# Attention of a one-core hybrid step: low scores over all 128 rows, value products of both heads side by side, context scores padded with zeros

## The chip, the cores and the metric

The kernel runs on one core of one Trainium2 chip. The metric is the device time in microseconds (us) of one execution, and the time of a kernel is the median of its runs. The engines are named as in the profile: PE is TensorE's matmuls, PEld its weight loads, DVE is VectorE, ACT is ScalarE, POOL is GpSimd and SP is SyncE, whose queue issues nearly all DMAs. A matmul has a stationary operand, which a weight load brings into the array, and a moving operand, whose columns are streamed through. The array has 128 rows (the contracted dimension) and 128 columns (the partitions of the output).

## The reference, cut to what matters

One inference step of a two-layer network over 512 latent tokens and 128 context tokens, D = 1024, everything in float32. Each layer is a half FFN, a token mixer and a half FFN. The mixer of layer 0 is a Fourier mixer, that of layer 1 is attention with 16 heads of 64 channels, and the change is in that attention alone.

```
q, k, v = split(h @ w_qkv)             # q scaled by 64 ** -0.5
# 128 context queries: dense over the 128 context keys of this step
p = softmax(q_ctx @ k_ctx.T);  o_ctx = p @ v_ctx
# 512 latent queries (grid of 8 rows x 64 columns): one softmax over
#   the 8 x 16 keys of the neighbourhood (plus a relative-position bias per head)
#   and the 128 cached context keys (no bias)
logits = concat([q @ k_win.T + bias, q @ cache_k.T])
o = softmax(logits) @ concat([v_win, cache_v])
```

The step also returns the context keys and values.

## The kernel before

**Layout.** Activations lie transposed: channels on the 128 partitions, tokens along the free dimension. The latent tokens are ordered column by column of the grid, so that a block of 128 neighbouring tokens needs the keys of two neighbouring 128-key tiles and the tile of cached keys: 384 keys in all, of which the bias masks those outside the window.

**Precision.** A float32 product of projections is three matmuls of a rounded kind (F32R, a reduced float32 that TensorE streams in one pass): an operand x is split into hi (x rounded) and lo (x minus hi), and `mm3` (lines 208 to 210) adds hi·hi, hi·lo and lo·hi. The split of a weight unit of 128x1024 is one ACT operation (L191) and one DVE operation (L193). Matmuls whose operands are plain F32 (transposes aside: values, context scores) show as two instructions each in the profile.

**The attention, stage by stage.** Heads are taken in eight pairs c; a pair has its 128 channels on the 128 partitions, head p0 = 0 on rows 0 to 63 and p0 = 1 on rows 64 to 127.

- `qk(c)` projects q and k of a pair: 4 x 8 triples of `mm3`, 320 columns each. `query` (L908, L916) and `key` (L933, L936) take the results out of PSUM. For head p0 the query tile holds the hi part on the head's own 64 rows and the lo part on the other 64. The key tile holds the hi part on the head's own rows, and `double` (L946) copies it to the other rows. So one matmul over 128 rows gives q_hi·k_hi + q_lo·k_hi. The lo part of the keys of both heads lies in one tile (`low`, the right part of `pair[0]`), on each head's own rows only.
- `v_tiles(quad, ts)` projects the values, 256 channels at a time; four quads, five token tiles each.
- `pair_parts(c, ...)` lists the work of a pair's attention as small parts. `scores(p0, b)` makes the scores of head p0 and query block b: the 128-row matmul L1038, then L1039, which takes q_hi (64 rows) with the lo keys (64 rows), both 384 columns into the same bank; then the softmax: L1042 on DVE (bias, maximum), L1024 DVE, L1025 ACT (exponential and its sum), L1026 and L1027 DVE. `turn` transposes the 128x384 weights in three steps on TensorE (L1052) into the one `turn` bank, and ACT copies them out (L1054). `values(p0, b)` (L1065) multiplies them with the values: stationary 128x64, so 64 columns of the array, the half that belongs to the head. `ctx_scores` (L1073, 64 rows) and `ctx_values` (L1088) do the same for the context queries.

**Order.** In `before` the jobs of a pair are the four blocks of head 0, the four of head 1, then the two of the context; at each step of the list stand the scores of job n, the turn of job n-1 and the values of job n-2, thirty parts in all. `weave` spreads the parts of pair c over the `mm3` triples of the projections of pair c+1 (and of a value quad, after c = 0, 3 and 5): `tick` adds a nominal time for each triple and takes the next part when its due time has come; `flush` emits what is left. After the flush `behind` appends three or four jobs of the modulation of later layers: each loads a 128x1024 tile and runs two products over it on DVE (L348). The last pair is woven into the first part of the output projection. The framework writes all waits and sets the order of each engine's queue; every engine takes its queue in order.

**Buffers that matter here.** PSUM: four `main` banks, two `score`, one `turn`, one `sum` (where the values of a pair are summed, and taken out by L1068 and L1090). SBUF: four `left` (softmax), three `right` (transposed weights), and four `raw` tiles, through which every weight unit, every modulation tile and every bias tile (L1032, `raw_tile`) passes. The DMA of a raw tile is issued on SP at L156 when its buffer is free.

Of the kernel before, what the change touches and what calls it, by code (L numbers as in the profile page):

```python
# [18 lines left out]
P = 128  # L19
# [28 lines left out]
TEMPS = {"square": (2, TOK), "total": (2, TOK), "rms": (2, HALF), "left": (4, 384), "right": (3, 384)}  # L48
# [9 lines left out]
KL = 512  # L58
QUERY_SEGS = (((0, HALF, 64),), ((HALF, 448, HALF + 64), (448, LAT, 0)))
KEY_SEGS = (((0, 256, 0), (256, HALF, 640)), ((HALF, 384, 640 + HALF - 256), (384, LAT, 512)))  # L60
BLOCK_KEYS = (slice(0, 5, 2), slice(0, 3), slice(1, 6, 2), slice(5, 2, -1))
BLOCK_BIAS = (slice(0, 7, 3), slice(1, 4), slice(1, 6, 2), slice(1, 4))
TAKEN = (
    ((0, 448, 64, ((1, None), (2, 3))), (64, 0, 64, ((0, 0), (1, None)))),
    ((0, 64, P, ((0, 0), (1, 1), (2, None))),),
    ((0, 192, P, ((0, 1), (1, None), (2, 2))),),
    ((0, 320, P, ((0, 2), (1, 3), (2, None))),),
# [11 lines left out]
def queries(pair, p0):  # L79
    return pair[1][:, 768:] if p0 else pair[0][:, :LAT]  # L80
# [29 lines left out]
class Kernel:  # L110
# [296 lines left out]
    def inverse_rms(self, acc):  # L407

        nc = self.nc
        final = type(acc) is list  # L410
        if not final:
            spare = acc[:, 1, :1]
            nc.vector.tensor_tensor(acc[:, 0], acc[:, 0], acc[:, 1], op=ALU.add)
            acc = [acc[:, 0]]
        nc.scalar.activation(self.col(1), acc[0][:, :1] if final else spare, AF.Sqrt)
        if not final:
            yield 1800
        in_turn = lambda: self.tc.issue_after(self.latest.ins) if self.latest else ExitStack()
        ps = self.bank("sum")
        cuts = (0, P, HALF - P)  # L420
        with in_turn():
            for j, t in enumerate(cuts):
                nc.tensor.matmul(ps[:, j : j + 1], acc[0][:, t : t + P], self.ones[:, :1], start=True, stop=True)  # L423
        col = self.col(3)
        nc.scalar.activation(col, ps[:, :3], AF.Sqrt, bias=self.eps, scale=1.0 / D)
        nc.vector.reciprocal(col, col)
        yield 1800
        ps = self.bank("sum")
        with in_turn():
            for j, t in enumerate(cuts):  # L430
                self.spread = nc.tensor.matmul(ps[:, t : t + P], col[:, j : j + 1].to_broadcast([P, P]), self.ident,  # L431
                                               start=True, stop=True)
        r = self.temp("rms")
# [455 lines left out]
    def attention(self, base, boundary):  # L889
# [13 lines left out]
        def query(c, half, ps):  # L903
# [6 lines left out]
            if half:  # L910
                ctx_qk[c] = self.temp("rms")
                nc.scalar.activation(ctx_qk[c][:, :P], ps[:, LAT - HALF : HALF], AF.Copy, scale=HD ** -0.5)
# [6 lines left out]
        def cached(c):  # L919
            low = pairs[c][0][:, KL:]  # L920
            for p0, (rows, other) in enumerate(sides):
                cache = self.cache[0][rows, c * P : (c + 1) * P].unsqueeze(1).to_broadcast([64, 2, P])
                two = lambda t: t[rows, 2 * P : 4 * P].rearrange("p (c t) -> p c t", c=2)
                k = two(pairs[c][1 + p0])
                nc.scalar.activation(k, cache, AF.Copy)
                nc.gpsimd.tensor_tensor(two(low), cache, k.bitcast(F32), op=ALU.subtract)

        def key(c, half, ps):
            low, *ks = pairs[c]
# [4 lines left out]
            for lo, hi, to in KEY_SEGS[half]:  # L934
                for p0, (rows, other) in enumerate(sides):
                    nc.vector.tensor_tensor(low[rows, KL + to : KL + to + hi - lo], ps[rows, lo - base : hi - base],  # L936
                                            ks[p0][rows, to : to + hi - lo].bitcast(F32), op=ALU.subtract)
            if half:
                kx = ctx_qk[c][:, P : 2 * P]
# [3 lines left out]
        def double(c):  # L943
            for p0, (rows, other) in enumerate(sides):
                k = pairs[c][1 + p0]
                nc.vector.tensor_copy(k[other, :768], k[rows, :768])  # L946
# [11 lines left out]
        def v_tiles(quad, ts, at=at):  # L958
# [4 lines left out]
            for t in ts:  # L963
                ps = self.bank("main" if quad else "score")
# [10 lines left out]
        for half in (0, 1):  # L975
# [38 lines left out]
    def pair_parts(self, c, pair, qk, v):  # L1014
# [14 lines left out]
        def scores(p0, b):  # L1029
            rows = slice(64 * p0, 64 * p0 + 64)  # L1030
            if b == 0:
                state["bm"] = self.raw_tile(io["bias"][2 * c + p0], BM)  # L1032
# [4 lines left out]
            hi, lo = tiles(ks[p0][:, :768]), tiles(pair[0][:, KL:])  # L1037
            nc.tensor.matmul(o, q, hi[:, BLOCK_KEYS[b]], start=True, stop=False)  # L1038
            nc.tensor.matmul(o, q[rows], lo[rows, BLOCK_KEYS[b]], start=False, stop=True)  # L1039
            L = self.temp("left")  # L1040
            mx = self.col(1)
            nc.vector.tensor_tensor_reduce(out=tiles(L), in0=o, in1=tiles(state["bm"])[:, BLOCK_BIAS[b]],  # L1042
# [14 lines left out]
        def values(p0, b):  # L1057
            ptb = state.pop(("t", (p0, b)))
            if p0 == 0 and b == 0:
                state["o"] = self.bank("sum")  # L1060
            ds = slice(64 * p0, 64 * p0 + 64)
            for at, q0, nq, tiles in TAKEN[b]:
                o = state["o"][ds, q0 : q0 + nq]
                for n, (i, k) in enumerate(tiles):
                    nc.tensor.matmul(o, cache_v[:, ds] if k is None else v[:, k, ds],  # L1065
                                     ptb[:, i * P + at : i * P + at + nq], start=n == 0, stop=n == len(tiles) - 1)
            if p0 == 1 and b == 3:
                nc.vector.tensor_copy(self.y[:, c, :LAT], state["o"])  # L1068

        def ctx_scores(p0):  # L1070
            rows = slice(64 * p0, 64 * p0 + 64)
            ps = self.bank("score")
            nc.tensor.matmul(ps[:, :P], qk[rows, :P], qk[rows, P : 2 * P],  # L1073
                             start=True, stop=True)
# [5 lines left out]
            state["c", p0] = L  # L1080

        def ctx_values(p0):
            ptb = state.pop(("t", ("c", p0)))
            if p0 == 0:
                state["o"] = self.bank("sum")
            o = state["o"]
            ds = slice(64 * p0, 64 * p0 + 64)
            nc.tensor.matmul(o[ds, :P], v[:, 4, ds], ptb[:, :P], start=True, stop=True)  # L1088
            if p0 == 1:
                nc.vector.tensor_copy(self.y[:, c, LAT:], o[:, :P])  # L1090

        jobs = []
        for p0 in range(2):
            for b in range(4):
                jobs.append((lambda p0=p0, b=b: scores(p0, b), lambda p0=p0, b=b: turn((p0, b), 384),
                             lambda p0=p0, b=b: values(p0, b)))
        for p0 in range(2):
            jobs.append((lambda p0=p0: ctx_scores(p0), lambda p0=p0: turn(("c", p0), P), lambda p0=p0: ctx_values(p0)))
        parts = []
        for n in range(len(jobs) + 2):  # L1100
            for stage in range(3):
                if 0 <= n - stage < len(jobs):
                    parts.append(jobs[n - stage][stage])
# [44 lines left out]
def host_inputs(x_prompt, x_sample, cache_k, cache_v, c, c_ctx, w_mod, b_mod, norm_pre, norm_post,  # L1148
# [39 lines left out]
    bm[:, :, 384:512] = 0.0  # L1188
    for qi in range(P):
        row = qi % ROWS  # L1190
        end = (48, (768,), 56 + qi // ROWS) if qi < 64 else (0, (0,), qi // ROWS - 8)
        for key0, tiles, col in (end, (0, (128, 256), 8 + qi // ROWS), (0, (128, 640), 8 + qi // ROWS)):
# [55 lines left out]
```

## Time and profile before

| | before |
|---|---|
| median of 3 runs | 2403.11 us (2402.08 to 2403.11) |
| the profiled execution | 2403.8 us; span 2402.0 us |
| granted TensorE clock, mean | 0.992 |
| PE busy / PEld busy | 97% / 94% of the span |
| DVE / ACT / POOL busy | 72% / 53% / 2% |
| stage from the first attention score to the last value copy | 1617.0 to 1897.4 us, 280.4 us |

The span runs from the first to the last instruction, and 1.8 us of the profiled execution lie outside it. "Busy" of an engine is time covered by at least one of its instructions. A matmul's duration in the groups contains its latency; matmuls are pipelined, so the time that one takes from the next is seen in the distance between starts, or in the chain of waits, which gives each piece of work the time by which it moved the end on.

### The profile page before, as it was taken

To read this page: it belongs to the slowest core of one execution; us is meant where nothing else is said; L and a number is where in the kernel's file an instruction comes from. 1 tells how busy PE (TensorE), PEld (TensorE's weight loads), DVE (VectorE), ACT (ScalarE), POOL (GpSimd) and SP (SyncE) were. 2 spreads that over 40 slices of the span, in tenths; PEclk is the share of its full clock that TensorE was granted. 3 is DMA by queue.
4 is the path that set the end of the run, shared out by engine and by line. 5 is a ranking of instruction groups with operands and counts; after the bars stand their busy time and mean duration, and the time that the engine had idled before them with its cause. 6 is when DMAs were issued, how large, how long until landed. Compare 5 with 4: busy or idle time off the path is not lost.

```text
span 2402.0 us, 39473 instructions
## 1 busy us (share of the span) xinstructions
PE 2339.2 (97%) x15692; PEld 2264.2 (94%) x15692; DVE 1740.3 (72%) x3112; ACT 1275.4 (53%) x2436; POOL 48.3 (2%) x34
## 2 busy tenths in 40 slices
PE   6999999998999999999999999999999999999997
PEld 5899999998999999999999999997888899999997
DVE  7788878389788887838878885577777586665553
ACT  3445545564664554557445554745445574545545
POOL 3200000000000000000000000000000000000000
PEclk9899999999999999999999999999999999999998
DMA  7134344334523434443333444223333222322231
GB/s 260 58 124 149 119 132 136 116 100 132 158 90 120 143 114 132 132 132 106 113 123 109 139 150 158 71 77 118 123 113 124 66 102 71 97 78 64 88 133 44
DMA packets 80140, 277.09 MB, mean 115 GB/s; under 512 B 8786, under 2 KB 15186, under 8 KB 79956
## 3 DMA queue, kind: packets, MB, share of 16 engines
q1 hardware_dynamic: 79684, 274.25, 35.4%
q8 instruction: 123, 2.02, 0.3%
q14 instruction: 61, 0.50, 0.1%
q10 hardware_dynamic: 272, 0.33, 0.0%
HBM read 263.00 MB, written 11.53 MB: 114 GB/s over the span
## 4 chain that ended last, share of the span: by engine, by line
PE 88%; DVE 5%; ACT 3%; DMA 2%; issue 1%; POOL 0%; SPq 0%; ACTq 0%; DVEq 0%
PE main L208 25%; PE main L210 25%; PE main L209 25%; PE score L208 2%; PE score L209 2%; PE score L210 2%; PE sum L1065 2%; DVE junk L348 1%; PE turn L1052 1%; PE score L1039 1%; ACT hi L191 1%; DVE lo L193 1%; DVE ring L203 1%; PE sum L431 1%; PE sum L423 1%
## 5 line engine op out<-in xcount | busy, mean ns | idle before, releaser
L208 PE MATMUL main<-ring,hi 128*128 128x320 f32 x3872 | 1202.9, 312 | 19.4 <-ACT ring L202 18.1
L209 PE MATMUL main<-ring,hi 128*128 128x320 f32 x3872 | 1205.0, 311 | 1.6 <-DVE ring L203 1.5
L210 PE MATMUL main<-ring,lo 128*128 128x320 f32 x3872 | 1204.3, 311 | 2.3 <-POOL lo L193 2.3
L208 PEld LDWEIGHTS main<-ring,hi 128*128 128x128 f32 x3872 | 729.1, 189 | 28.6 <-ACT ring L202 20.5
L209 PEld LDWEIGHTS main<-ring,hi 128*128 128x128 f32 x3872 | 731.1, 189 | 7.0 <-DVE ring L203 3.6
L210 PEld LDWEIGHTS main<-ring,lo 128*128 128x128 f32 x3872 | 730.9, 189 | 5.8 <-POOL lo L193 2.8
L191 ACT ACTIVATE hi<-raw 128x1024 fp32r<-128x1024 f32 (+1 forms) x358 | 350.6, 982 | 476.1 <-PE main L209 382.3
L193 DVE TENSOR_TENSOR lo<-raw,hi 128x1024 fp32r<-128x1024 f32 (+1 forms) x354 | 398.1, 1125 | 163.7 <-ACT hi L191 162.9
L348 DVE SCALAR_TENSOR_TENSOR junk<-raw,wide 128x1024 bf16<-128x1024 f32 x256 | 312.8, 1222 | 16.8 <-DMA raw<-in_w_mod_t 14.4
L643 ACT ACTIVATE y<-main 128x320 f32<-128x320 f32 x320 | 137.9, 432 | 174.2 <-PE main L210 173.0
L384 DVE TENSOR_TENSOR total<-total,square 128x640 f32<-128x640 f32 x71 | 58.3, 823 | 115.8 <-ACT square L383 114.8
L631 ACT ACTIVATE main<-y 128x320 f32<-128x320 f32 x256 | 111.8, 439 | 23.5 <-DVE left L617 10.0
L209 PE MATMUL score<-ring,hi 128*128 128x320 f32 x384 | 118.7, 309 | 0.0
L208 PE MATMUL score<-ring,hi 128*128 128x320 f32 x384 | 118.7, 310 | 0.0
L210 PE MATMUL score<-ring,lo 128*128 128x320 f32 x384 | 118.6, 309 | 0.0
L193 DVE TENSOR_TENSOR lo<-sums,hi 128x1024 fp32r<-128x1024 f32 x64 | 78.2, 1222 | 52.5 <-ACT hi L191 52.5
L210 PE MATMUL main<-ring,ring 128*128 128x320 f32 x352 | 110.0, 313 | 5.8 <-POOL ring L193 5.8
L208 PE MATMUL main<-ring,ring 128*128 128x320 f32 x352 | 111.4, 317 | 0.0
L209 PE MATMUL main<-ring,ring 128*128 128x320 f32 x352 | 109.6, 312 | 0.0
L191 ACT ACTIVATE hi<-sums 128x1024 fp32r<-128x1024 f32 x64 | 67.9, 1061 | 28.0 <-PE main L209 20.5
L1054 ACT ACTIVATE right<-turn 128x384 f32<-128x384 f32 (+1 forms) x80 | 35.8, 448 | 84.5 <-PE turn L1052 84.3
L202 ACT ACTIVATE ring<-right 128x320 fp32r<-128x320 f32 x112 | 51.6, 468 | 46.2 <-DVE right L530 37.7
(195 smaller groups left out, 2820.6 us busy)
## 6 DMA issues: line engine op xcount, KB each, us to landing
raw<-in_w SPq DMA_DIRECT2D x264, 512.0 KB, 3.6
raw<-in_w_mod_t SPq DMA_DIRECT2D x128, 512.0 KB, 3.7
raw<-in_qkv SPq DMA_DIRECT2D x26, 512.0 KB, 3.6
spill<-ring SPq DMA_DIRECT2D x12, 640.0 KB, 3.4
ring<-spill SPq DMA_DIRECT2D x12, 640.0 KB, 4.8
raw<-in_bias SPq DMA_DIRECT2D x16, 448.0 KB, 3.3
first<-in_w_mod_t SPq DMA_DIRECT2D x8, 512.0 KB, 10.2
raw<-in_four_in SPq DMA_DIRECT2D x8, 512.0 KB, 3.6
```

The source lines that it names most:

```text
L191: nc.scalar.activation(hi, raw[:, at], AF.Copy)
L193: engine.tensor_tensor(lo, raw[:, at], hi.bitcast(F32), op=ALU.subtract)
L202: self.nc.scalar.activation(hi, src, AF.Copy)
L208: mm(out, whi, xhi, start=start, stop=False)
L209: mm(out, whi, xlo, start=False, stop=False)
L210: self.latest = mm(out, wlo, xhi, start=False, stop=stop)
L348: last = self.nc.vector.scalar_tensor_tensor(out=self.junk, in0=raw, scalar=1.0, in1=self.wide[:, cond, :], op0=ALU.mult, op1=ALU.mult, ac ...
L384: nc.vector.tensor_tensor(acc, acc, sq, op=ALU.add)
L631: nc.scalar.activation(ps[:, :HALF], self.y[:, m, lo:hi], AF.Copy)
L643: nc.scalar.activation(self.y[:, m, lo:hi], ps[:, :HALF], AF.Copy)
L1054: nc.scalar.activation(ptb[:, :w], pt[:, :w], AF.Copy)
L1065: nc.tensor.matmul(o, cache_v[:, ds] if k is None else v[:, k, ds], ptb[:, i * P + at : i * P + at + nq], start=n == 0, stop=n == len(tile ...
```

## The change

1. **Scores.** The lo keys of a head move from the common tile into the head's own key tile (columns 640 to 1279, behind its hi keys), and `double` copies hi and lo to the other 64 rows, 1280 columns in place of 768. The second score matmul then contracts over 128 rows, with the same stationary query tile as the first. The cached keys are stored once instead of twice (five 128-key tiles instead of six), the tile order and the bias layout follow. Both heads' queries go side by side into `pair[0]`.
2. **Values.** `values(b)` does block b of both heads: for each key tile, head 0's matmul (output partitions 0 to 63), then head 1's (64 to 127), alternating.
3. **Context scores.** The context queries of each head get their own 128 columns with zeros (memset on POOL) on the other head's 64 rows, and the matmul contracts over 128 rows. The `rms` tiles grow from 320 to 384 columns for this.
4. **Order.** A pair's blocks are 0, 1, 2, 3, context; at each step stand the scores of block n for both heads, the values of block n-2, the turns of block n-1 for both heads: 25 parts. Both bias tiles of the pair are loaded at block 0.
5. **Banks.** The first tiles of value quad 1 (before the second half's projections) use `score` banks in place of `main`.

```diff
-KL = 512
+KL = 640
...
-BLOCK_KEYS = (slice(0, 5, 2), slice(0, 3), slice(1, 6, 2), slice(5, 2, -1))
+BLOCK_KEYS = (slice(0, 3), slice(3, 0, -1), slice(2, 5), slice(0, 5, 2))
...
 def queries(pair, p0):
-    return pair[1][:, 768:] if p0 else pair[0][:, :LAT]
+
+    return pair[0][:, p0 * LAT : (p0 + 1) * LAT]
...
             if half:
                 ctx_qk[c] = self.temp("rms")
-                nc.scalar.activation(ctx_qk[c][:, :P], ps[:, LAT - HALF : HALF], AF.Copy, scale=HD ** -0.5)
+                for p0, (rows, other) in enumerate(sides):
+                    q = ctx_qk[c][:, p0 * P : (p0 + 1) * P]
+                    nc.gpsimd.memset(q[other], 0.0)
+                    nc.scalar.activation(q[rows], ps[rows, LAT - HALF : HALF], AF.Copy, scale=HD ** -0.5)
...
         def cached(c):
-            low = pairs[c][0][:, KL:]
             for p0, (rows, other) in enumerate(sides):
-                cache = self.cache[0][rows, c * P : (c + 1) * P].unsqueeze(1).to_broadcast([64, 2, P])
-                two = lambda t: t[rows, 2 * P : 4 * P].rearrange("p (c t) -> p c t", c=2)
-                k = two(pairs[c][1 + p0])
-                nc.scalar.activation(k, cache, AF.Copy)
-                nc.gpsimd.tensor_tensor(two(low), cache, k.bitcast(F32), op=ALU.subtract)
+                cache = self.cache[0][rows, c * P : (c + 1) * P]
+                k = pairs[c][1 + p0][rows]
+                nc.scalar.activation(k[:, 2 * P : 3 * P], cache, AF.Copy)
+                nc.gpsimd.tensor_tensor(k[:, KL + 2 * P : KL + 3 * P], cache, k[:, 2 * P : 3 * P].bitcast(F32),
+                                        op=ALU.subtract)
...
         def double(c):
+
             for p0, (rows, other) in enumerate(sides):
                 k = pairs[c][1 + p0]
-                nc.vector.tensor_copy(k[other, :768], k[rows, :768])
+                nc.vector.tensor_copy(k[other], k[rows])
...
-                ps = self.bank("main" if quad else "score")
+                ps = self.bank(bank)
...
-                v_tiles(quad, ((0, 1), (2, 3, 4))[half], at if half else early)
+                v_tiles(quad, ((0, 1), (2, 3, 4))[half], at if half else early, "score")
...
             if b == 0:
-                state["bm"] = self.raw_tile(io["bias"][2 * c + p0], BM)
+                state["bm", p0] = self.raw_tile(io["bias"][2 * c + p0], BM)
...
-            nc.tensor.matmul(o, q, hi[:, BLOCK_KEYS[b]], start=True, stop=False)
-            nc.tensor.matmul(o, q[rows], lo[rows, BLOCK_KEYS[b]], start=False, stop=True)
+            for part in range(2):
+                nc.tensor.matmul(o, q, tiles(ks[p0])[:, 5 * part : 5 * part + 5][:, BLOCK_KEYS[b]],
+                                 start=part == 0, stop=part == 1)
...
-        def values(p0, b):
-            ptb = state.pop(("t", (p0, b)))
-            if p0 == 0 and b == 0:
+        def values(b):
+
+            ptb = [state.pop(("t", (p0, b))) for p0 in range(2)]
+            if b in (0, "c"):
                 state["o"] = self.bank("sum")
-            ds = slice(64 * p0, 64 * p0 + 64)
-            for at, q0, nq, tiles in TAKEN[b]:
-                o = state["o"][ds, q0 : q0 + nq]
+            taken = ((0, 0, P, ((0, 4),)),) if b == "c" else TAKEN[b]
+            for at, q0, nq, tiles in taken:
                 for n, (i, k) in enumerate(tiles):
-                    nc.tensor.matmul(o, cache_v[:, ds] if k is None else v[:, k, ds],
-                                     ptb[:, i * P + at : i * P + at + nq], start=n == 0, stop=n == len(tiles) - 1)
-            if p0 == 1 and b == 3:
+                    for p0 in range(2):
+                        ds = slice(64 * p0, 64 * p0 + 64)
+                        nc.tensor.matmul(state["o"][ds, q0 : q0 + nq], cache_v[:, ds] if k is None else v[:, k, ds],
+                                         ptb[p0][:, i * P + at : i * P + at + nq], start=n == 0,
+                                         stop=n == len(tiles) - 1)
...
-            nc.tensor.matmul(ps[:, :P], qk[rows, :P], qk[rows, P : 2 * P],
-                             start=True, stop=True)
+            nc.tensor.matmul(ps[:, :P], qk[:, p0 * P : (p0 + 1) * P], qk[:, 2 * P :], start=True, stop=True)
...
+        blocks = [0, 1, 2, 3, "c"]
+        both = lambda do: [partial(do, p0) for p0 in range(2)]
         parts = []
...
+        for n in range(len(blocks) + 2):
+            if n < len(blocks):
+                b = blocks[n]
+                parts += both(ctx_scores if b == "c" else lambda p0, b=b: scores(p0, b))
+            if n >= 2:
+                parts.append(partial(values, blocks[n - 2]))
+            if 1 <= n <= len(blocks):
+                b = blocks[n - 1]
+                parts += both(lambda p0, b=b: turn((p0, b), P if b == "c" else 384))
         return parts
```

More of the change, by code (lines that the diff above doesn't have):

```diff
@@ L1079, in ctx_scores @@
             softmax(L, mx, P)
[L1080 to L1098, printed above, removed]
[L1099 to L1103 removed]
+            state[p0, "c"] = L
+        blocks = [0, 1, 2, 3, "c"]
+        both = lambda do: [partial(do, p0) for p0 in range(2)]
+        parts = []
+        for n in range(len(blocks) + 2):
[7 more added lines that the diff above has]
+                parts += both(lambda p0, b=b: turn((p0, b), P if b == "c" else 384))
         return parts
```

38 lines of the change are left out of this document (19 added, 19 removed).

## The prediction

> **What bounds the kernel now.** I read the page first, then a table of stretches to find the stage, then its waits and its chain.
>
> ```profile
> span 2402.0 us, 39473 instructions
> PE 88%; DVE 5%; ACT 3%; DMA 2%; issue 1%; POOL 0%; SPq 0%; ACTq 0%; DVEq 0%
> ```
>
> TensorE carries 88% of the chain that ended last. The attention lies between its first score at 1617.0 us and its last value copy at 1897.4. For that stretch the table of stretches has one row (columns: stretch, length, then busy time with the number of instructions of PE, PEld, DVE, ACT and POOL, clock, DMA):
>
> ```profile
> 1617.00:1897.40 280.40, 277.39 (x1759) 221.84 (x1757) 210.53 (x670) 141.51 (x380) 9.31 (x12) 1.00 0.38 119
> ```
>
> PE is busy 277.4 of 280.4 us at full clock, DVE 210.5 (75%), ACT half. So every us that TensorE's queue loses here comes off the end, until DVE at 210.5 becomes the bound. That limit lies only 70 us below, and it decides the size of this change.
>
> How long TensorE is held by each kind of work is read from the chain of waits (start, time by which the piece moved the end on, what):
>
> ```profile
> 1661.73 0.15 PE main L208
> 1661.87 0.17 PE score L1038
> 1662.05 0.36 PE score L1039
> 1662.41 0.35 PE main L209
> ...
> 1663.05 0.33 PE turn L1052 x3
> ```
>
> A projection matmul in a steady stream costs 0.15, the score matmul on 128 rows 0.17. The 64-row one streams the same 384 columns and costs 0.36, and the matmul behind it 0.35 in place of 0.15. The extra 0.19 and 0.20 are paid at the change from 128 rows to 64 and back: TensorE stops overlapping there. The transposes, on the whole array, cost 0.11 each.
>
> ```profile
> 1664.26 0.80 PE sum L1065 x6
> ...
> 1669.76 0.61 PE sum L1065 x8
> 1670.37 0.35 PE main L210
> ...
> 1671.16 0.41 PE score L1073 x2
> 1671.57 0.48 PE turn L1052 x3
> ```
>
> A block's value products of one head cost 0.80 (three products of 128 queries, two instructions each) or 0.61 (block 0: four of 64 queries), and the matmul behind them again 0.20 too much. The context score of a head costs 0.41 for two instructions, and the transposes behind it 0.15 more than their 0.33. The context values of one head are the pair
>
> ```profile
> 1650.69 0.42 PE sum L1088 x2
> 1651.11 0.34 PE main L210
> ```
>
> **The change part by part.**
>
> *Scores.* A block costs 0.17 + 0.36 + (0.35 - 0.15) = 0.73 now. On 128 rows the second matmul is of the first one's form, 0.17, and nothing is paid behind it: 0.34. That saves 0.39 a block. The projections' first two matmuls also share a stationary operand and each loads it, so I count no saved load. 16 heads x 4 blocks x 0.39 = **25.0 us**.
>
> *Context scores.* 0.41 + 0.48 becomes two instructions at the transposes' 0.11 and three transposes at 0.33, that is 0.55: 0.34 saved, times 16 = **5.4 us**.
>
> *Value products.* Here the question is whether matmuls on the left and the right 64 columns run at the same time. Attention before never has them next to each other, but the Fourier stage does (instructions in order of time: start, duration):
>
> ```profile
> 568.34 0.32 PE L839 MATMUL turn<-ring,y 128*64 128x128 f32 x1
> 568.35 0.32 PE L840 MATMUL turn<-ring,ring 128*63 128x128 f32 x1
> 568.50 0.27 PE L839 MATMUL turn<-ring,y 128*64 128x128 f32 x1
> 568.51 0.27 PE L840 MATMUL turn<-ring,ring 128*63 128x128 f32 x1
> 568.71 0.38 PE L836 MATMUL score<-ring,y 128*128 128x128 f32 x1
> ```
>
> L839 writes partitions 0 to 63, L840 64 to 126, each a plain-float32 product of 128 columns in two instructions. They start 0.01 apart, and four instructions are through in 0.37 us, less than the 0.42 that two of one head cost above. So I take the second head as free. It costs now, per pair, 3 x (0.80 + 0.20) + (0.61 + 0.20) = 3.81 for the latent blocks and 0.42 + 0.19 = 0.61 for the context; 8 x 4.42 = **35.4 us**. The bound from the other side, no overlap in a longer run of twelve, leaves only the merged groups: five exits of 0.20 a pair, 8 us.
>
> There is a rule against this. The Trainium skill ("TensorE: Matmul & The Clock Gate", Part 3, "The mechanism") says that a weight load overlaps with matmuls in flight only when its row group differs, and both halves use all rows; by it the second head saves nothing, and the loads come on top. The rows above speak against it here, since four loads and four matmuls fit into 0.37 us. It stays as a rival below.
>
> *TensorE's sum.* 25.0 + 5.4 + 35.4 = 65.8 us; the stage would take 280.4 - 65.8 = 214.6 if nothing else held it.
>
> *DVE.* Its work stays but for `double`:
>
> ```profile
> L946 DVE CAST ring<-ring 64x768 fp32r<-64x768 f32 x12 | 6.7, 555 | 0.4
> L1024 DVE TENSOR_SCALAR col<-col 128x1 f32<-128x1 f32 x80 | 11.6, 145 | 0.4
> ```
>
> 1280 columns cost at most 555 x 1280 / 768 = 925 ns, and at least 145 + (555 - 145) x 1280 / 768 = 828 if a column-free part as large as the smallest operation's stands in it: 12 x 0.27 to 0.37, so 4 us. DVE then has 214.5 us to do in a stage of 214.6. Both engines cannot be full to the last us, so something is given back. What DVE waits for is, beside TensorE's results, which come earlier now, ACT (total, times, longest):
>
> ```profile
> DVE col L1026 <- ACT left L1025: 12.6, 19, 1.2
> DVE ring L936 <- ACT ring L933: 10.3, 11, 1.2
> DVE ring L916 <- ACT rms L912: 6.9, 5, 2.3
> DVE ring L916 <- ACT ring L908: 4.6, 3, 2.6
> ...
> DVE ring L193 <- ACT ring L191: 1.9, 2, 1.3
> ...
> DVE lo L193 <- ACT hi L191: 1.5, 2, 0.9
> ```
>
> That is 37.8 us. Below it lies full filling (nothing given back: the modulation products take the gaps), above it none (all 37.8). That DVE can be nearly full beside a full TensorE is shown elsewhere in this kernel:
>
> ```profile
> 1340.00:1360.00 20.00, 20.00 (x139) 20.00 (x138) 19.37 (x35) 13.12 (x27) 0.00 (x0) 1.00 0.48 158
> ```
>
> There 19.37 of 20 us, but with long independent operations; the softmax passes from DVE to ACT and back in every block. I take half: 18.9 us. The stage then takes 214.5 + 18.9 = 233.4, **47.0 us** less than now.
>
> *What costs nothing.* The extra ACT copy of the context queries and the shorter one of the cached keys are covered by ACT's idle half, the memsets by POOL's 271 idle us; uncovered, the memsets would hold the context scores, the last block of a pair, not the first. Reversed and moved key tiles stream the same 384 columns. The early `score` banks remove one wait of TensorE for a `main` bank and let the next quad wait for a `score` bank instead, whose copy is queued on DVE:
>
> ```profile
> 1575.29 0.36 PE L208 MATMUL main<-hi,ring 128*128 128x256 f32 x1 [1.47 <-DVE ring L916]
> ```
>
> So plus or minus 1.5 us, taken as nothing.
>
> *What is moved.* Both bias tiles are loaded at block 0 and held until block 3, so two of four `raw` tiles are pinned for most of a pair where one was. SP takes its queue in order, and the second bias load now stands ahead of weight units and modulation tiles:
>
> ```profile
> SPq L156 <- DVE junk L348: 58.4, 11, 10.8
> raw<-in_bias SPq DMA_DIRECT2D x16, 448.0 KB, 3.3
> L348 DVE SCALAR_TENSOR_TENSOR junk<-raw,wide 128x1024 bf16<-128x1024 f32 x48 | 58.8, 1225 | 1.3 <-DMA raw<-in_w_mod_t 1.3
> ```
>
> SP already waits for modulation products to free a tile. The second bias tile needs one job more to end, 2 x 1.225 = 2.45 us, before head 1's first score can be used; over the seven pairs that follow such jobs, 0 to 17 us. TensorE has that pair's projections to run meanwhile, so I count 0 and keep 17 for the range.
>
> The two turns of a block now stand next to each other and share the one `turn` bank, so the second needs ACT's copy of the first:
>
> ```profile
> L1054 ACT ACTIVATE right<-turn 128x384 f32<-128x384 f32 x64 | 31.4, 490 | 56.6 <-PE turn L1052 56.4
> PE turn L1052 <- ACT right L1054: 0.3, 1, 0.3
> ```
>
> The parts are still spread over projection triples of 3 x 0.15 = 0.45, so about that much stands between the two turns; what is left is counted in the half of ACT's waits.
>
> *Sum.* 2403.8 (the profiled execution) - 47.0 = 2356.8. That execution lies 0.7 above the median of 2403.11, so 2356.1 on its scale: **2356 us**.
>
> **The rivals.**
>
> *A. TensorE's whole gain arrives* (DVE's gaps are filled): 2403.1 - 65.8 = 2337. For it, the stretch with DVE at 97%; against it, two full engines at once for 215 us.
>
> *B. The feeds bind* (none of ACT's waits filled): 2403.1 - 65.8 + 37.8 = 2375, with bias tiles late up to 17 more, 2392. For it, SP's wait and the pinned tiles; against it, TensorE lost only 3 us in this stage so far.
>
> *C. The halves don't run side by side in a long run*, the part of the change that may not do what it says: 25.0 + 5.4 + 8 = 38.4, TensorE stays the bound, 2365. Against it, L839 and L840.
>
> *D. Slower: the one `turn` bank.* If ACT has queued the next block's two exponentials ahead of the copy of the first turn, and TensorE's queue has no triples between the two turns, TensorE stands for
>
> ```profile
> L1025 ACT ACTIVATE left<-left,col 128x384 f32<-128x384 f32 x64 | 39.2, 613 | 24.7 <-DVE col L1024 22.5 <-DVE mod L363 1.7
> L1025 ACT ACTIVATION_READ_ACCUMULATOR left<-left,col 128x1 f32 x64 | 12.0, 188 | 0.0
> ```
>
> two exponentials with their sums, 2 x 0.80, and the copy of 0.49: 2.1 us a block, 40 blocks, 84 us. 2403 - 66 + 84 = 2421. It decides from 65.8 / 40 = 1.65 us a block on. Against it: the triples between the parts, and the 0.3 us that the bank has cost so far.
>
> *E. Slower by exposed loads*, the skill's rule taken at its word. The load of 64 columns takes
>
> ```profile
> L1065 PEld LDWEIGHTS sum<-right,ring 128*64 128x64 f32 x160 | 18.0, 137 | 2.9 <-issue 1.2 <-ACT right L1054 1.0 <-ACT ring L925 0.2
> ```
>
> 0.137, a product's instruction 0.80 / 6 = 0.13. If every load waits for the other half's matmul, a block of both heads takes 12 x 0.27 = 3.2 in place of 2.0, block 0 16 x (0.137 + 0.08) = 3.5 in place of 1.6, a pair 5.5 more: +44 against -30.4, 2417. Against it, the same five rows of the Fourier stage.
>
> *F. No change*, 2403: only if D's wait came to just 1.65 us a block.
>
> **How the numbers follow.** Forecast 0.60 (own range 2346 to 2368: a fifth to four fifths of ACT's waits filled, the banks' 1.5), A 0.15, B 0.15, C 0.04, D 0.03, E 0.01, F 0.02. The range reaches down to A, 2336, and up through B with half of the bias price, 2384; D, E, F and the upper end of B are left out. Faster by over 0.2% (about what a measurement of this kernel can tell from no change, 5 us) are the forecast, A, B and C: 0.94; same 0.02, slower 0.04.
>
> **What would show it.** The score matmuls would show one form of 128 rows, 128 in number, at 0.17 in the chain, with 0.15 for the matmul behind them; wrong if 0.36 and 0.35 remain. The value products would start in pairs 0.01 apart, a block of both heads in 0.8 us; wrong, and C or E, if it takes 1.6 or more. DVE would be busy over 90% of a stage of about 233 us, and TensorE's idle time in it would grow from 3 to about 19 us, with DVE and ACT named as releasers; with A it stays under 5, with B the raw tiles' DMAs or SP stand in its waits, with D the turn's wait for L1054 is the longest. The prediction fails if the stage's length is set by one of these or if the other stages move by more than 3 us.

## The result, and the profile after

The changed kernel takes 2377.36 us (median of 4 runs, 2376.43 to 2378.5) against 2402.6 us in the same comparison: a ratio of 0.9897 (95% interval 0.9879 to 0.9914), 25.2 us or 1.0% less. The forecast was 2356, in a range of 2336 to 2384. So the direction and the range held, and little more than half of the forecast 47 us came. The narrower range of the forecast's own case, 2346 to 2368, was missed by 9 us.

The page of the changed kernel has this span and this chain (shares by engine):

```profile
span 2374.6 us, 39530 instructions
PE 87%; DVE 5%; ACT 4%; issue 2%; DMA 1%; POOL 0%; SPq 0%; ACTq 0%; DVEq 0%
```

The stage now runs from its first score at 1620.5 to the last value copy at 1871.0. The table of stretches (length, then busy PE, PEld, DVE, ACT, POOL, clock, DMA):

```profile
1620.50:1871.00 250.50, 239.51 (x1744) 205.49 (x1744) 212.57 (x669) 141.47 (x386) 10.05 (x24) 0.99 0.42 133
```

It is 250.5 us long where it was 280.4; 3 us are lost ahead of it. (In the trace of the kernel before, the first score starts at 1617.48, so that its stage is 280.1 us when counted as here, from the start of the first score.) TensorE is busy for 239.5, not for the 214.6 of my sum, and idle for 11.0 where it was idle for 3.0. DVE is busy 85%. Neither engine is full: so the missing us lie first in TensorE's own work. The chain of waits of the changed kernel (start, time by which it moved the end on, what) shows what that work costs:

```profile
1662.34 0.36 PE sum L1070 x2
1662.70 0.35 PE main L210
...
1663.34 0.35 PE score L1041 x2
1663.69 0.33 PE turn L1055 x3
...
1664.74 0.80 PE sum L1070 x10
1665.55 0.35 PE main L209
```

The scores are as forecast: two matmuls on 128 rows in 0.35 us, and the transposes behind them at their undisturbed 0.33. The value products of a block are not one group of twelve instructions in 0.80 us. They are a lone product of two instructions (0.36, and 0.20 too much behind it) and, a few matmuls later, the other ten in 0.80. The order of TensorE's queue, read from the built program, shows why (place, line, out from stationary and moving operands; the two `right` tiles are the heads' transposed weights):

```
10548 L1070 MATMUL sum_16879<-right_16976,ring_15811 64x128
10549 L209 MATMUL main_17316<-ring_15737,hi_16751 128x320
...
10554 L1055 MATMUL turn_16981<-ident,left_16868 128x128 x3
...
10562 L1070 MATMUL sum_16879<-right_16985,ring_15811 64x128
10563 L1070 MATMUL sum_16879<-right_16976,total_16110 64x128
10564 L1070 MATMUL sum_16879<-right_16985,total_16110 64x128
```

The first product needs head 0's weights alone (`right_16976`). It is put into the queue as soon as they are there; head 1's turn (place 10554) comes only six places later, and its weights (`right_16985`) later still. Projections fill the place in between. Over the whole queue the value products form 79 groups, 41 of them a single product. The kernel before had 80. Of the 40 blocks of the changed kernel all 32 latent ones and five of the eight context blocks are split.

### The profile page after: what moved, and what is told of

Same layout as the page of the kernel before. It is cut to its first block, busy times and chain, and to the rows that moved or that the text cites. A ratio compares the mean times of both kernels' runs of the same rounds, so it can differ in the third digit from the quotient of the medians.

```text
span 2374.6 us, 39530 instructions
## 1 busy us (share of the span) xinstructions
PE 2302.0 (97%) x15692; PEld 2249.1 (95%) x15692; DVE 1743.5 (73%) x3112; ACT 1277.0 (54%) x2444; POOL 48.8 (2%) x50
## 4 chain that ended last, share of the span: by engine, by line
PE 87%; DVE 5%; ACT 4%; issue 2%; DMA 1%; POOL 0%; SPq 0%; ACTq 0%; DVEq 0%
PE main L209 25%; PE main L211 25%; PE main L210 25%; PE score L209 2%; PE score L210 2%; PE score L211 2%; PE sum L1070 2%; DVE junk L349 1%; ACT hi L192 1%; PE turn L1055 1%; PE score L1041 1%; DVE lo L194 1%; PE sum L432 1%; DVE ring L204 1%; ACT right L1057 1%
## 5 line engine op out<-in xcount | busy, mean ns | idle before, releaser
L604 DVE TENSOR_TENSOR left<-left,main 128x320 f32<-128x320 f32 x64 | 31.2, 487 | 59.6 <-PE main L211 59.6
## 6 DMA issues: line engine op xcount, KB each, us to landing
first<-in_w_mod_t SPq DMA_DIRECT2D x8, 512.0 KB, 10.2
```

Source lines behind the costliest of these rows:

```text
L604: tt(a, q, z, op=ALU.subtract)
```

## The experiments

Each is an edit of the changed kernel, or of an experiment named. Ratios are to the kernel before, with 95% intervals. A stage runs from the start of the kernel's first score to the end of its last value copy. The expectation for half of the modulation counts its stage of 235 us from 2.1 us earlier, among the projections; from the first score it is 233.1.

**Head 1 first.** The product that is ready last goes ahead, so that no other can leave without it: 42 groups.

```diff
                 for n, (i, k) in enumerate(tiles):
-                    for p0 in range(2):
+                    for p0 in (1, 0):
```

> The changed kernel, but in every value product the matmul of head 1, whose transposed weights are ready last, stands ahead of that of head 0, so that no product can start before both heads' weights are there. In the order of TensorE's queue the value products form 42 groups in place of 79 (41 of them a single product). Theory, the gain was lost to split groups: in the chain of the changed kernel a lone product costs 0.36 us and the matmul behind it 0.20 too much, 0.56 us for each of 40 blocks, 22 us; the time falls from 2377 to about 2355, to 2360 if DVE's and ACT's results come late for part of it. Rival, the stage is held by ACT and DVE (TensorE's idle time in it is 11.6 us against 3.0 before): the time stays within 5 us of 2377 and TensorE's idle time grows by about what the groups save.

Measured: 2363.61 us, 0.9835 (0.9821 to 0.985), 13.8 us less than the changed kernel. Its chain and its stage:

```profile
1661.04 0.81 PE sum L1070 x12
...
1620.82:1853.90 233.08, 223.06 (x1742) 198.43 (x1741) 212.37 (x669) 141.89 (x385) 10.94 (x24) 0.99 0.45 143
```

The twelve instructions of both heads now take 0.81 us, as forecast. The stage is 17.4 us shorter: TensorE's busy time falls by 16.4 us, and its idle time from 11.0 to 10.0; the rival, that idle time would take up what the groups save, falls. The 22 us expected were too many, since the queue has 37 groups fewer and not 40: 37 x 0.56 = 20.7. The stage of 233.1 us is within 0.5 us of the 233.4 that the prediction had for it, with DVE at 91%.

Of the 17.4 us, 14.5 reach the end of the profiled execution, because 2.6 are lost again behind the stage. TensorE's short waits pile up at the stage's end (it is busy for 1.82 of the 3.41 us before 1852.15), and its clock is then at half for 6.8 us, where in the changed kernel it is at full speed:

```profile
1852.15:1858.98 6.83, 6.46 (x25) 5.84 (x26) 1.22 (x4) 4.38 (x11) 0.00 (x0) 0.50 0.00 0
```

**Heads in sequence** inside a group, and **the same half** for both, test whether the halves really run side by side.

```diff
-                for n, (i, k) in enumerate(tiles):
-                    for p0 in (1, 0):
+                for p0 in (1, 0):
+                    for n, (i, k) in enumerate(tiles):
...
-                        nc.tensor.matmul(state["o"][ds, q0 : q0 + nq], ...
+                        nc.tensor.matmul(state["o"][:64, q0 : q0 + nq], ...   (second kernel only)
```

> As the kernel with head 1 first, with the same number of groups (42), but in each group all products of head 1 come first, then all of head 0: no alternation of the column halves. Theory, the halves overlap only where neighbours in the queue are of different halves: a block's group then takes about 1.45 to 1.6 us in place of 0.80, 0.65 to 0.8 us more for 32 latent blocks and 0.25 for 8 context blocks, so 23 to 28 us above the kernel with head 1 first, about 2380. Rival, TensorE runs the halves side by side whatever the order inside a group: no difference to the kernel with head 1 first.

> The kernel with the heads in sequence inside a group (2364.7 us, ratio 0.9839), with the products of both heads sent to the same 64 output partitions, so that they can't run side by side (it leaves out the output of half of the partitions; the copies out take 64 partitions). 50 groups in place of 42, 8 x 0.56 = 4.5 us more. Theory, the overlap of the halves is what the other 0.65 us of a block come from: a group of 12 takes 1.45 us in place of 0.80 to 1.07; 32 x 0.5 + 8 x 0.2 + 4.5 = 22 us more by TensorE's queue, of which two thirds to all arrive: 2380 to 2387. Rival, merged groups alone made the gain and the halves don't overlap in a long run: not above 2370.

Measured: heads in sequence 2364.72 us, 0.9839 (0.9823 to 0.9856); the same half 2375.72 us, 0.9889 (0.9874 to 0.9903). A group of twelve in the chain of the first, then of the second:

```profile
1663.66 1.07 PE sum L1070 x12
```

```profile
1674.86 1.52 PE sum L1070 x12
```

Alternating 0.81, in sequence 1.07, on one half 1.52. So the halves do overlap in a long run, and the order inside a group counts for little: 1.1 us between the medians and 4.1 in the traced stages (237.2 against 233.1), where 23 to 28 were expected. The instructions of the kernel with heads in sequence, in order of time:

```profile
1663.60 0.43 PE L1070 MATMUL sum<-right,total 128*64 128x128 f32 x2
1663.86 0.27 PE L1070 MATMUL sum<-right,ring 128*64 128x128 f32 x1
1663.87 0.32 PE L1070 MATMUL sum<-right,total 128*64 128x128 f32 x1
```

0.27 us after the group's start there are already pairs 0.01 apart, although in the queue head 0's first product stands behind three of head 1 (for each head: `total`, `ring`, `total`, two instructions each). The theory that only neighbours overlap falls. Without overlap the kernel loses 11.0 us, not 22: TensorE's busy time in its stage is 12.5 us longer. Part of that is that some groups are split between the heads: its trace has 14 runs of six instructions, that of heads in sequence has one.

**Heads apart**: value products as one part of the list per head, 81 groups, no overlap.

```diff
-                parts.append(partial(values, blocks[n - 2]))
+                b = blocks[n - 2]
+                parts += both(lambda p0, b=b: values(p0, b))
```

> The changed kernel, with the value products of the two heads as two parts of the list, as the kernel before had them: no alternation at all, 81 groups. Theory, what alternation gave in the changed kernel as built is 2 x (0.80 + 0.20) = 2.0 us against 0.36 + 0.20 + 0.80 + 0.20 = 1.56 us for a latent block of 128 queries, 0.44 for 24 blocks, about the same for the 16 others: 14 to 18 us back, 2391 to 2395. Rival, alternation gave nothing as built since the stage is held elsewhere: within 5 us of 2377.

Measured: 2389.61 us, 0.9944 (0.9929 to 0.9959), 12.2 us more than the changed kernel and 26.0 more than head 1 first. So joining the heads' products was worth 26 us in this kernel, and the change as built took 12 of them.

**Low scores on 64 rows** again, the rest left as changed.

```diff
-            for part in range(2):
-                nc.tensor.matmul(o, q, tiles(ks[p0])[:, 5 * part : 5 * part + 5][:, BLOCK_KEYS[b]], ...)
+            nc.tensor.matmul(o, q, k[:, :5][:, BLOCK_KEYS[b]], start=True, stop=False)
+            nc.tensor.matmul(o, q[rows], k[rows, 5:10][:, BLOCK_KEYS[b]], start=False, stop=True)
```

> The changed kernel, with the second score matmul on the head's own 64 rows again (it leaves out the product of the lo queries with the lo keys, as the kernel before did). Everything else, the layout and the longer copy of the keys on DVE included, stays. Theory, TensorE bounds the stage and each change between 128 and 64 rows costs 0.19 to 0.20 us: 64 x 0.39 = 25 us back, 2402. Rival, the stage is held by ACT and DVE: less than half of that, under 2390, because TensorE's idle time (11.6 us) takes it up.

Measured: 2394.18 us, 0.9963 (0.995 to 0.9976), 16.8 us more than the changed kernel. Chain and stage:

```profile
1660.52 0.17 PE score L1042
1660.69 0.37 PE score L1043
1661.06 0.48 PE turn L1056 x3
...
1619.72:1888.00 268.28, 261.11 (x1743) 208.03 (x1742) 213.37 (x669) 141.21 (x385) 9.01 (x24) 0.98 0.40 124
```

The old prices are back: 0.37 for the 64-row matmul, 0.15 too much behind it. TensorE's busy time rises by 21.7 us, where 25 were counted; its idle time falls by 3.8, the stage is 17.9 us longer, and 16.8 us arrive. Up to 3.4 of the 21.7 come from the clock, which is at half for 10.2 us of this stage and for 3.4 us of the changed kernel's. The result lies between the two expectations, nearer to the rival's bound of 2390 than to the theory's 2402: most of what the queue loses arrives, not all.

**Context scores on 64 rows** again.

```diff
-            nc.tensor.matmul(ps[:, :P], qk[:, p0 * P : (p0 + 1) * P], qk[:, 2 * P :], start=True, stop=True)
+            nc.tensor.matmul(ps[:, :P], qk[rows, p0 * P : (p0 + 1) * P], qk[rows, 2 * P :], start=True, stop=True)
```

> The changed kernel (2377.4 us), with the context scores on the head's own 64 rows again; the zeros are still written. Theory, two changes of the row count for each of 16 products cost 0.34 us together: 5.4 us if all of it comes through, 3.7 if the share is that of the latent scores (17 of 25 us): 2381 to 2383. Rival, the context stands at the end of a pair where TensorE waits anyway: within 1 us of 2377.4.

Measured: 2379.36 us, 0.9906 (0.9892 to 0.9921), 2.0 us more than the changed kernel, in intervals that overlap. The price in the queue is the old one:

```profile
1672.03 0.42 PE score L1081 x2
```

TensorE is busy 4.6 us longer in the stage (5.4 were counted), about 2 reach the end, less than the theory's 3.7, and the run doesn't tell 2 from nothing.

**Early tiles in main banks**, on head 1 first.

```diff
-                v_tiles(quad, ((0, 1), (2, 3, 4))[half], at if half else early, "score")
+                v_tiles(quad, ((0, 1), (2, 3, 4))[half], at if half else early, "main" if quad else "score")
```

> The kernel with head 1 first (2363.6 us), with the early tiles of value quad 1 in main banks again, as in the kernel before. Between 1570 us and the first attention score TensorE idled 2.5 us before the change and 4.9 us after it. Theory, the move to score banks put that loss there (the norm's small matmul waits 2.8 us for DVE in place of a main bank's 2.4): 2 to 3 us less, about 2361. Rival, the idle time there has to do with the longer key copy or the zero fill and stays: no difference above 1 us.

Measured: 2357.99 us, 0.9815 (0.98 to 0.9829), 5.6 us less by the medians and 4.8 by the ratios, twice what was expected. In the traces the first score comes 3.7 us earlier (at 1617.1) and the stage is as long as before (232.9 us). The stretches of the changed kernel, then of this one, show it (columns as above; the clock is the last but two):

```profile
1575.00:1580.00 5.00, 2.90 (x25) 2.69 (x23) 4.82 (x11) 3.79 (x6) 0.00 (x0) 1.00 0.00 0
1580.00:1585.00 5.00, 3.43 (x18) 3.41 (x19) 2.94 (x9) 0.70 (x2) 0.00 (x0) 0.71 0.65 191
1585.00:1590.00 5.00, 5.00 (x42) 5.00 (x41) 4.73 (x11) 3.59 (x7) 0.00 (x0) 0.95 0.05 20
```

```profile
1575.00:1580.00 5.00, 4.69 (x40) 4.51 (x39) 4.81 (x12) 3.06 (x5) 0.00 (x0) 1.00 0.01 3
1580.00:1585.00 5.00, 4.91 (x41) 4.70 (x41) 3.56 (x8) 1.40 (x5) 0.00 (x0) 1.00 0.65 197
```

With the early tiles in the two score banks TensorE runs dry, and the clock falls to 0.71 over the five us after the pause and 0.95 over the next five. The instructions of the changed kernel there:

```profile
1580.71 0.80 PE L424 MATMUL sum<-ones,total 128*128 128x1 f32 x6 [2.81 <-DVE total L414]
...
1584.42 0.41 PE L209 MATMUL score<-hi,ring 128*128 128x256 f32 x1
1584.63 0.41 PE L210 MATMUL score<-lo,ring 128*128 128x256 f32 x1
...
1586.00 0.28 PE L209 MATMUL score<-hi,ring 128*128 128x256 f32 x1
1586.12 0.28 PE L210 MATMUL score<-lo,ring 128*128 128x256 f32 x1
```

A pause of 2.81 us, then matmuls 0.21 apart in place of 0.12 until 1585.5. I had taken the banks as nothing, with a bound of 1.5 either way.

**Half of the modulation products** left out of the stage, on head 1 first.

```diff
-                        self.gemv(self.raw_tile(self.io["w_mod_t"][layer, j]), layer, j)
+                        self.gemv(self.raw_tile(self.io["w_mod_t"][layer, j]), layer, j, (0,) if self.woven_stage else (0, 1))
```

> The kernel with head 1 first, with half of the modulation products that stand in the attention left out (24 of 48 of 128x1024, those of the context condition; it leaves out that part of the modulation of layer 1). Their loads stay. DVE has 24 x 1.22 = 29 us less to do in a stage of 235 us in which it is busy for 214 and TensorE idles for 10. Theory, what the stage still lacks against TensorE's own 225 us is DVE's fullness: 5 to 9 us less, 2355 to 2359. Rival, it is the latency of the softmax chain through ACT, whatever DVE's load: within 2 us of 2363.6.

Measured: 2355.81 us, 0.9808 (0.9793 to 0.9822), 7.8 us less by the medians, 6.5 by the ratios. The stage:

```profile
1622.76:1852.10 229.34, 220.01 (x1744) 196.79 (x1743) 189.72 (x616) 140.72 (x385) 8.62 (x24) 1.00 0.46 145
```

The time is what the theory gave, the trace only half of it: DVE has 22.6 us less to do, but TensorE still idles for 9.3 us, and the stage is 3.7 us shorter. The two profiled executions differ by 4.4 us, and 2.6 of them lie behind the stage, where this kernel's clock is full and that of head 1 first was at half. So DVE's fullness costs at most some us, and is not what most of TensorE's remaining idle time comes from.

**Turns apart**: the values' part goes between the two turns of a step, on head 1 first.

```diff
+            parts += turns[:1]
             if n >= 2:
                 parts.append(partial(values, blocks[n - 2]))
+            parts += turns[1:]
```

> The kernel with head 1 first, with the part for the values between the two turns of a step, so that the two turns don't follow each other at the one turn bank and the values come one part later. It has 48 groups of value products in place of 42, 6 x 0.56 = 3 us more. Theory, TensorE's remaining idle time is the wait for ACT's copies of the turned weights (4.3 us before value products, 2.1 before turns): up to 6 us less, net 2358 to 2364. Rival, the copies are late because ACT's exponentials wait for DVE, and the order of the turns doesn't matter: 2364 to 2368.

Measured: 2359.75 us, 0.9821 (0.9805 to 0.9837), 3.4 to 3.9 us less, inside the theory's band, though the intervals overlap and the stage in the trace is not shorter (233.8 against 233.1): TensorE idles 1.8 us less in it and is busy 2.4 us longer, as the six groups more would have it. What the profiled execution gains, 1.5 us, lies behind the stage, so the theory's reason is not shown.

**Three mends** together, and on top of them **a third pinned tile** and **values taken out by ACT**.

```diff
# a third pinned tile
+                if p0 == 1:
+                    state["pin"] = self.raw.tile([P, UNIT], F32, tag="raw", name=self.name("pin"))
+                    nc.gpsimd.memset(state["pin"][:, :8], 0.0)
...
+            if b == 3 and p0 == 1:
+                nc.vector.tensor_copy(self.col(8), state["pin"][:, :8])
# values taken out by ACT
-                    nc.vector.tensor_copy(v[:, t, :], ps[:, i * P : (i + 1) * P])
+                    nc.scalar.activation(v[:, t, :], ps[:, i * P : (i + 1) * P], AF.Copy)
```

> Head 1 first, the values' part between the two turns, and main banks for the early tiles of quad 1, all three together. If the gains of the last two against the kernel with head 1 first (4.8 and 3.4 us by their ratios to the kernel before: 0.9815 and 0.9821 against 0.9835) add up: 0.9801, 2354 us. If they are the same gain (TensorE idle time that DVE's fullness gives back): 0.981 to 0.982, 2357 to 2359.

> The kernel with three mends, in which a pair pins one raw tile more from block 0 to block 3 (three of four in place of two). Theory, the raw tiles already bind: with one tile for weights and modulation, each passing in 3.6 + 1.06 + 1.22 = 5.9 us, 48 tiles of the stage need over 235 us for the pinned four fifths of it: 20 to 60 us slower. Rival, the loads run so far ahead that even one tile is enough: under 8 us slower. The result says how near the two pinned tiles of the change are to a bound.

> The kernel with three mends, with the projected values taken out of PSUM by ACT in place of DVE: 80 copies of 0.28 us in the whole attention, 64 of them (18 us) in the woven stage, move from DVE (91% busy there) to ACT (61%). Theory, DVE's fullness holds the rest, at the rate seen when half of the modulation was left out (6.5 us of 29): 3 to 4 us less than with three mends. Rival, ACT's queue delays the copies of turned weights and softmax for which TensorE waits: the same or 1 to 4 us more.

Measured: three mends 2356.83 us, 0.9809 (0.9794 to 0.9824); with the third pin 2364.71, 0.984 (0.9826 to 0.9855); with the values on ACT 2356.44, 0.9806 (0.9789 to 0.9822). Whether the gains of the last two of the three mends add up (0.9801) or are one gain (0.981 to 0.982), the interval doesn't tell. In the trace their stage of 233.6 us is no shorter than the 233.1 with head 1 first; it starts 3.4 us earlier. The third pin costs 7.9 us, just under the rival's limit. The stage of the three mends, then with the third pin:

```profile
1617.41:1851.00 233.59, 225.32 (x1744) 200.06 (x1743) 212.31 (x669) 141.44 (x386) 11.90 (x24) 0.99 0.46 143
```

```profile
1619.41:1859.70 240.29, 224.53 (x1743) 199.75 (x1742) 214.12 (x676) 140.46 (x385) 10.15 (x31) 0.99 0.44 139
```

TensorE's idle time rises from 8.3 to 15.8 us: the third pinned tile of four costs something. Whether the second does was not run. For the values on ACT the expectation counted more than twice the copies there are (the trace before has 40 in all, not 80, and 26 in the woven stage, not 64), so 1 to 2 us were to be had at most; nothing shows.

The fastest kernels, main banks for the early tiles, three mends, and these with the values on ACT, can't be told apart at 0.9806 to 0.9815. All beat both kernels: 45 us under the kernel before, 20 under the changed one.

## Why the prediction was right, and where its size was off

- **What bounds the stage** was right. TensorE's lost time decides: 21.7 us more in its queue cost 16.8 at the end, 16.4 less gave 13.8.
- **Scores, 25.0 us**: right in the queue (0.35 for both matmuls, nothing behind them); undoing it gives TensorE 21.7 us more to do.
- **Context scores, 5.4 us**: nearly right in the queue (4.6), but not at the end (2.0, unclear).
- **Value products, 35.4 us**: the step that was mis-sized. "I take the second head as free" was right of the hardware (0.81 us for both heads). But the sum also took each block's instructions for one group, and as built nearly every block is two: 37 groups too many (all 32 latent blocks and five of the context), by the chain 0.36 + 0.20 for each lone product, 20.7 of the 35.4 us. Putting head 1 first returned 17.4 us in the stage and 13.8 at the end. Whole groups against none (head 1 first against heads apart) are worth 31.8 us of TensorE's busy time and 26.0 at the end, so even then the term of 35.4 was somewhat too large. I had looked at how the two turns share a bank, and not asked which of the two heads' weights the first product needs and what the queue does until the others come.
- **`double` on DVE**: bounded at 828 to 925 ns. Measured

```profile
L950 DVE CAST ring<-ring 64x1280 fp32r<-64x1280 f32 x12 | 9.9, 822 | 0.4
```

  6 ns under the lower bound; the term of 4 us stands at 3.2.
- **18.9 us given back**: this rested on DVE at 214.5 us standing beside TensorE at 214.6. In the changed kernel TensorE had more to do and DVE was 85% busy, not over 90%, so little was due for that reason; still 8 us of new idle time came, most of it here (total, times, longest):

```profile
PE sum L1070 <- ACT right L1057: 6.5, 14, 1.0
```

  With the groups mended the stage took 233.1 us against the forecast 233.4, but by another split: TensorE's busy time was 223.1 in place of 214.6 and its idle time 10.0 in place of 18.9. The agreement of the total is luck: one term was 8.5 us too small, the other 8.9 too large. Half was a choice without a measurement behind it, and the half modulation shows that DVE's load is not the main cause of the idle time.
- **The early banks, taken as nothing**: wrong, they cost 4.8 to 5.6 us.
- **The raw tiles, counted as 0 of 17**: no wait of TensorE in the changed kernel's stage names them, which fits; one pin against two was not run. A third costs 7.9.
- **The rivals**: the halves do overlap (against C), and the whole gain (A), the slow bank (D) and the exposed loads (E) did not happen. The time fell near B's 2375, for another reason than B's: no wait of TensorE names the loads or the second bias tile, and the split groups decided. That the result fell inside the outer range, whose upper end was B's, is luck too: no rival had the split groups.

From forecast to result, in the profiled executions: 27.4 us came (span 2402.0 to 2374.6) where 47.0 were forecast. The stage went from 280.1 to 250.4 us, 29.7 less and 17.3 short of the forecast; head 1 first takes 17.4 off it, so what the stage lacked is what the split groups cost. Ahead of the stage 3.1 us were lost, by the early banks (main banks return 3.7), and behind it 0.8 were gained: 47.0 - 17.3 - 3.1 + 0.8 = 27.4. The prediction's bound of 3 us for other stages was thus just passed. Of the 10 us of idle time that stay with head 1 first, TensorE's waits put 6.4 down to ACT's copies of the turned weights; what makes these late is open, and DVE's load is at most part of it.

## What to carry to other kernels

A saving that depends on several small matmuls standing together in TensorE's queue is only there if the first of them can't leave before the last is ready: let the first one wait for the input that comes last, and count the groups in the queue's order. Price a merged group from the chain with the exit that stands behind it, since the exit (0.20 us here) costs nearly as much as a product (0.27, a third of 0.80). And look at a moved bank for the pause it makes, not only for the wait it removes.

## What the hardware showed beyond the expected

- Products on the two column halves run side by side even when they don't alternate: in sequence 1.07 us for twelve instructions, alternating 0.81, on one half 1.52. TensorE takes matmuls of the other half past those that stand ahead of them, so here its queue is in order only within a half. The Trainium skill ("TensorE: Matmul & The Clock Gate", Part 3, "The mechanism") has matmuls strictly in order and loads overlapping only between different row groups; the rows of this case show neither for column halves.
- A pause of TensorE of 2.81 us, with one of 0.86 soon behind it, was enough to bring matmuls to about half speed (0.21 us apart in place of 0.12) for 3.4 us; in the kernel before, a single one of 2.24 us (from 1554.2) did the same. The Trainium skill's page "TensorE: Matmul & The Clock Gate" warns of idle gaps above about 3.4 us ("HAM oscillation — how this bites in real kernels") and says in Part 1 ("What's actually happening") that the window runs freely; this trace shows that a shorter pause can trip it.
- It need not be one pause. In the stage of the changed kernel three waits of 0.26, 0.96 and 0.93 us close together did the same (the first row has the 3.41 us before the clock fell, the second those after it):

```profile
1834.72:1838.13 3.41, 1.51 (x8) 0.84 (x7) 3.21 (x9) 2.64 (x5) 0.00 (x0) 1.00 0.40 147
1838.13:1841.54 3.41, 3.15 (x17) 2.35 (x17) 2.60 (x14) 1.41 (x5) 0.00 (x0) 0.50 0.32 87
```

  In the 14 traces of this case the clock keeps each value for 3.41 us or a multiple of it. From the first recorded change on, every such step of 3.41 us at full clock in which TensorE was busy for 1.75 us or less was followed by one at half clock, and none in which it was busy for over 1.87 us. So what counts here is TensorE's idle time within a step, about half of it, and not the length of one pause.
